# Storing zs before its silu and only q's rotated rows: a change to a one-core transformer-block kernel

## The chip, the cores and the metric

The kernel runs on one core of a Trainium2 chip. TensorE (PE) multiplies matrices, VectorE (DVE) and ScalarE (ACT) work element by element, GpSimd (POOL) mostly issues accumulating DMAs here, and SyncE (SP) issues most of the others; a DMA is carried by the core's 16 DMA engines. The metric is the device time of one execution in microseconds, the median of several runs: 925.65 us before the change.

## The reference

One block of a streaming encoder on 1024 tokens of width 1024, in float32. Cut to what matters (`h @ w_in` is split by columns into q, k, v, za, u, vs, zs and the gates gm):

```python
h = rmsnorm(x, norm_g)
q, k, v, za, u, vs, zs, gm = jnp.split(h @ w_in, IN_SPLITS, axis=-1)
q, k = partial_rope(q, pos), partial_rope(k, pos)   # rows 0..15 of each head's 64 turn, 16..63 stay
a = window_sink_attention(q, k, v, sinks)           # 16 heads of 64, 2 of them for k and v
a = (a * silu(za)) @ w_att_out
sgo = chunked_spatial_gating(gelu(u), gelu(vs), ...)
sgo = (sgo * silu(zs)) @ w_sg_out
ga, gs = jnp.split(sigmoid(gm + b_merge), 2, axis=-1)
x = rmsnorm(x + (ga * a + gs * sgo) @ w_o, final_g)
```

`partial_rope` takes x1 (the first eight rows of a head) and x2 (the next eight) and makes x1 cos - x2 sin and x2 cos + x1 sin.

## The kernel before, in words

Activations lie transposed: channels on the 128 partitions, tokens along the row, in two halves of 512. A big product is made in pairs of 128 channels (m and m + 1, m = 0, 2, 4, 6) by `gemm_pair`, which replaces eight block products by seven: b11, t1, t2, b21, t3, b22, t4 in this order. Each is 12 matmuls of 128x128 by 128x512, since every float32 operand is split into a high and a low part (`wh` on ACT, `wl` on DVE). Weights arrive as `wr`; their sums `s` are made on DVE (L242 to L245), one pair ahead, and split as well; t1 to t4 of the next pair need `wl<-s` and `wh<-s`. The results of a pair are four quarters x (128x512), put together on ACT (L359, L363, L366) and DVE (L371, L376, L380). `finish` is called for each quarter, and `hook` after each of the seven products: through hooks the side work (rotation, attention, loads ahead) is spread over the products. x tiles are reused, so a quarter must have left its tile before a later pair can fill it.

The stages in time: rmsnorm and vs (to about 100 us), u (107 to 218), k and v (218 to 238), q (four pairs, to 296), zs (four pairs, 296 to 429), gs and ga (eight pairs, to 610), za (four pairs, to 686), the product with w_sg_out (`sg`, to about 783), the product with w_att_out, the output product and the last norm.

**q.** `finish` puts each quarter twice: raw to `q_raw` in DRAM, and split into high and low parts (`split_q`, L880 on ACT, L882 on DVE) to `q_hl`, from where attention loads it. `rotate(g, pause)` does the 16 rotated rows for a group g of eight heads: it loads x1 and x2 from `q_raw` (L935, all eight heads, both halves of tokens, on 128 partitions), waits `1 + pause` hooks, multiplies by the tables (L955 to L957, L960 to L962) and puts the result over the rows in `q_hl` through `split_q`. Group 0 is rotated in the q pairs m = 4 and 6, group 1 in the first zs pair. `rotate` loads through SP's queue, which serves its issues in order; an issue that waits for a put to land holds up all that stand behind it.

**zs.** `zs_pair` collects the four raw quarters, then takes their silu on ACT (L1061), loads four factors of 256 KB from `s1_dr` (the mixed and gated branch, stored in the u stage), multiplies on DVE (L1071) and puts to `s_dr`. Attention runs beside the pairs m = 2, 4, 6 and beside gs and ga; its exponentials (L1120) and the silu use different activation tables on ACT, so ACT loads a table where they alternate (ACT_TABLE_LOAD). `exps` and `after` order silus behind the last exponentials.

**gs, ga.** They are stored by `rest(dst, m)`, which puts each raw quarter to `gs_dr` and `ga_dr` without activation.

**za.** `finish` takes the silu of each quarter (L1360), multiplies by a gate from `at_dr` (the attention's result, L1361) and puts to `a_dr`; four gates wait in the tag "g". From m = 2 on the four quarters of s (1 MB each) are loaded from `s_dr` into the tag "bq", and at m = 6 `forms_of` begins to make the operands T_ of the sg pairs from them on ACT and DVE.

Of the kernel before, what the change touches and what calls it, by code (L numbers as in the profile page):

```python
# [52 lines left out]
def hybrid_tile(  # L53
# [63 lines left out]
    q_raw = scratch("q_raw")  # L117
    q_hl = scratch("q_hl", (2, D, S))
# [4 lines left out]
    s_dr = scratch("s_dr")  # L123
# [751 lines left out]
    def split_q(src, places):  # L875

        hl = mtile([P, 2, HALF], F32R, "qhl", 3, pool)
        hi, lo = (hl[:, a, :].rearrange("p (t q c) -> p t c q", c=2, q=64) for a in range(2))
        src = src.rearrange("p (t c q) -> p t c q", c=2, q=64)
        nc.scalar.mul(hi, src, SC)  # L880
        for c in range(2):
            nc.vector.scalar_tensor_tensor(  # L882
                lo[:, :, c], src[:, :, c], SC, hi[:, :, c].bitcast(F32), op0=ALU.mult, op1=ALU.subtract
            )
        for at, dst in places:
            nc.sync.dma_start(dst, hl[at].bitcast(F32))
# [42 lines left out]
    def rotate(g, pause):  # L929

        x1, x2, a, b = (mtile([P, HALF], F32, "rot", 5, pool) for _ in range(4))
        for j, dst in enumerate((x1, x2)):
            src = q_raw[:].rearrange("(h d) t -> h d t", h=16)[8 * g : 8 * g + 8, 8 * j : 8 * j + 8]
            for half in range(2):
                nc.sync.dma_start(dst[halves[half]], src[:, :, half_of(half)])  # L935

        def split_rows(src, j):
# [4 lines left out]
                        (halves[half], a),  # L942
                        q_hl[a].rearrange("(h d) t -> h d t", h=16)[
                            8 * g : 8 * g + 8, 8 * j : 8 * j + 8, half_of(half)
                        ],
                    )
                    for a in range(2)
# [76 lines left out]
    def query_stage(g, t, par):  # L1024
# [3 lines left out]
        for j in range(2):  # L1028
            rows = q_hl[j].rearrange("(c r d) t -> r d c t", r=2, d=HD)[par]
            nc.sync.dma_start(  # L1030
                qt[j * HD : (j + 1) * HD].bitcast(F32), rows[:, 4 * g : 4 * g + 4, t * P : (t + 1) * P]
            )
# [3 lines left out]
    exps = []  # L1036
# [7 lines left out]
    def zs_pair(m, hook, *place, ahead_by=0):  # L1044
        quarters, fetched, hooked = [], [], [0]

        def fetch(i, half):
            fetched.append(get(s1_dr, m + i, half, *place))

        def step():  # L1050
            hook()
            hooked[0] += 1
            if hooked[0] == ahead_by:
                for at in ((0, 0), (1, 1)):
                    fetch(*at)

        gemm_pair(hb, lambda *quarter: quarters.append(quarter), step)

        first = None
        for i, half, q, src, sign in quarters:  # L1060
            silu = nc.scalar.activation(q[:], src, AF.Silu, scale=sign)  # L1061
            first = first or silu
            if silu is not first:
                after(silu, first)
            elif exps:
                after(silu, exps[-1])
        for i, half, q, src, sign in quarters:
            if not fetched:
                fetch(i, half)
            g = fetched.pop(0)  # L1070
            nc.vector.tensor_mul(q[:], q[:], g[:])  # L1071
# [17 lines left out]
    def softmax_stage(g, t, par, qt):  # L1089
# [40 lines left out]
        exps.append(nc.scalar.activation(es[:], es[:], AF.Exp))  # L1130
# [140 lines left out]
    QUARTERS = ((0, 0), (0, 1), (1, 0), (1, 1))  # L1271

    def loads_of_quarters(qs, src):


        def load(j, half):
            q = mtile([P, 4, HALF], F32, "bq", 4, pool)
# [23 lines left out]
    def load_o(name, wait=lambda move: None):  # L1301
        q = mtile([P, 4, HALF], F32, "bq", 4, pool)
# [41 lines left out]
    def want_gates(src, m):  # L1344
        for i, half in ORDER:
            gates.append(get(src, m + i, half, 4))


    for m in range(0, KC, 2):
        if m == 0:  # L1350
            want_gates(at_dr, m)
        if m == 2:
            s_q = {}
            ahead_of_time += loads_of_quarters(s_q, s_dr)
# [4 lines left out]
        def finish(i, half, q, src, sign):  # L1359
            nc.scalar.activation(q[:], src, AF.Silu, scale=sign)  # L1360
            nc.vector.tensor_mul(q[:], q[:], gates.pop(0)[:])  # L1361
# [4 lines left out]
        gemm_pair(hb, finish, part_of_loads, "tp")  # L1366
    want_gates(gs_dr, 0)
# [18 lines left out]
    for m in range(0, KC, 2):  # L1386
# [7 lines left out]
        def finish(i, half, q, src, sign):  # L1394
            gated(q, src, sign, gate_of(gs_dr, m, i, half, KC))
            put(y_dr, m + i, half, q[:], nc.gpsimd)
            gates.append(get(gs_dr, m + 2 + i, half, 4) if m < 6 else get(ga_dr, i, half, 4))
# [67 lines left out]
    for m in range(0, KC, 2):  # L1465
# [6 lines left out]
        def finish(i, half, q, src, sign):  # L1472
            gated(q, src, sign, gate_of(ga_dr, m, i, half, 0))
            if m < 6:
                add_to(place(y_dr, m + i, half), q[:])
                gates.append(get(ga_dr, m + 2 + i, half, 4))
# [23 lines left out]
    def load_rows(p):  # L1500
        xr = mtile([P, 4, HALF], F32, "bq", 4, pool)
# [6 lines left out]
    for p in range(4):  # L1508
        acc = bank("sc" if p < 2 else "mm")[:]
        x11 = mtile([P, HALF], F32, "g", 4, pool)  # L1510
# [5 lines left out]
    g_out = mtile([P, 4, HALF], F32, "bq", 4, pool)[:, 0:2, :]  # L1516
# [8 lines left out]
    for p in range(4):  # L1525
# [10 lines left out]
        def add_and_square(i, half, src, sign):  # L1536
# [4 lines left out]
            if p == 3 and i == half:  # L1541
                scaled[i, half] = mtile([P, HALF], F32, "g", 4, pool)
# [157 lines left out]
```

## Time and profile before

| | |
|---|---|
| median of 3 runs | 925.65 us (924.44 to 926.13) |
| the profiled execution | 928.16 us, of which the span of the profile is 926.4 us |
| TensorE's granted clock, mean | 0.994 of full speed |
| PE busy | 908.8 us (98%) |
| DVE, ACT, POOL busy | 691.7, 530.7, 127.0 us |
| chain that ended last | PE 79%, DVE 10%, ACT 4%, DMA 3% |
| DMA | 201.71 MB, mean 218 GB/s |

A row of a timeline reads: start and length in us, engine and line, operation, output<-input, shapes, count, and in brackets how long the engine stood idle before it and what it waited for. A row of waits reads: who waited, for whom, us in total, how many times, the longest. A granted clock of 1.00 is full speed; PE counts as busy at any clock. The share of DMA is a mean over the 16 engines.

### The profile page before, as it was taken

To read this page: it belongs to the slowest core of one execution; us is meant where nothing else is said; L and a number is where in the kernel's file an instruction comes from. 1 tells how busy PE (TensorE), PEld (TensorE's weight loads), DVE (VectorE), ACT (ScalarE), POOL (GpSimd) and SP (SyncE) were. 2 spreads that over 40 slices of the span, in tenths; PEclk is the share of its full clock that TensorE was granted. 3 is DMA by queue.
4 is the path that set the end of the run, shared out by engine and by line. 5 is a ranking of instruction groups with operands and counts; after the bars stand their busy time and mean duration, and the time that the engine had idled before them with its cause. 6 is when DMAs were issued, how large, how long until landed. Compare 5 with 4: busy or idle time off the path is not lost.

```text
span 926.4 us, 13211 instructions
## 1 busy us (share of the span) xinstructions
PE 908.8 (98%) x4332; PEld 754.6 (81%) x4332; DVE 691.7 (75%) x1245; ACT 530.7 (57%) x1057; POOL 127.0 (14%) x188
## 2 busy tenths in 40 slices
PE   8999999999999999999999999999999999999996
PEld 6888888888888778788888888888887887888885
DVE  6774776656687578888878888746498589579996
ACT  6862443334455468887666676744475475467443
POOL 0002122213021001101111121001100111110012
PEclk9999999999999989999999999999999999999999
DMA  6427678777788777888687789779668764998632
GB/s 239 136 90 208 208 199 182 164 157 233 231 294 269 210 222 196 223 212 231 188 228 258 233 175 258 209 263 323 217 199 325 256 197 151 298 313 282 205 114 114
DMA packets 128830, 201.71 MB, mean 218 GB/s; under 512 B 12441, under 2 KB 60825, under 8 KB 128762
## 3 DMA queue, kind: packets, MB, share of 16 engines
q1 hardware_dynamic: 109608, 148.17, 49.3%
q0 software_dynamic: 19008, 52.44, 23.6%
q8 instruction: 34, 0.56, 0.2%
q14 instruction: 34, 0.28, 0.1%
q10 hardware_dynamic: 146, 0.27, 0.1%
HBM read 144.07 MB, written 86.11 MB: 248 GB/s over the span
## 4 chain that ended last, share of the span: by engine, by line
PE 79%; DVE 10%; ACT 4%; DMA 3%; issue 3%; SPq 1%; DVEq 0%; ACTq 0%
PE ps_mm L341 32%; PE ps_o L341 23%; PE ps_mm L596 5%; PE ps_sc L1107 3%; PE ps_tp L341 2%; DVE wl L156 2%; PE ps_o L1192 2%; PE ps_sc L341 2%; PE ps_tp L1151 2%; PE ps_tp L764 2%; DVE bq L185 1%; PE ps_tp L565 1%; PE ps_sc L565 1%; PE ps_o L565 1%; PE ps_mm L565 1%
## 5 line engine op out<-in xcount | busy, mean ns | idle before, releaser
L155 ACT CAST wh<-s 128x1024 fp32r<-128x1024 f32 (+1 forms) x78 | 78.1, 1005 | 89.7 <-PE ps_mm L341 44.5
L156 DVE TENSOR_TENSOR wl<-wr,wh 128x1024 fp32r<-128x1024 f32 (+1 forms) x80 | 75.7, 947 | 56.0 <-ACT wh L155 55.3
L155 ACT CAST wh<-wr 128x1024 fp32r<-128x1024 f32 (+1 forms) x80 | 66.3, 830 | 76.1 <-PE ps_mm L341 37.3
L156 DVE TENSOR_TENSOR wl<-s,wh 128x1024 fp32r<-128x1024 f32 (+1 forms) x78 | 90.8, 1166 | 9.9 <-ACT wh L155 9.9
L341 PE MATMUL ps_o<-T_b22h,wh 128*128 128x512 f32 x148 | 58.7, 396 | 2.0 <-ACT x L363 2.0
L341 PE MATMUL ps_o<-T_t1h,wh 128*128 128x512 f32 x148 | 58.9, 398 | 0.3 <-ACT wh L155 0.2
L341 PE MATMUL ps_o<-T_b22h,wl 128*128 128x512 f32 x148 | 58.0, 392 | 0.0
L341 PE MATMUL ps_o<-T_t1h,wl 128*128 128x512 f32 x148 | 57.8, 391 | 0.2 <-DVE wl L156 0.2
L341 PE MATMUL ps_o<-T_b22l,wh 128*128 128x512 f32 x148 | 57.9, 391 | 0.0
L341 PE MATMUL ps_o<-T_t1l,wh 128*128 128x512 f32 x148 | 57.7, 390 | 0.0
L341 PE MATMUL ps_mm<-T_b11h,wl 128*128 128x512 f32 x140 | 54.8, 392 | 2.1 <-DVE wl L156 2.1
L341 PE MATMUL ps_mm<-T_t4h,wh 128*128 128x512 f32 x140 | 55.2, 394 | 1.1 <-DVE x L376 0.9
L341 PE MATMUL ps_mm<-T_t2h,wh 128*128 128x512 f32 x140 | 54.9, 392 | 1.2 <-ACT x L359 1.2
L341 PE MATMUL ps_mm<-T_t3h,wh 128*128 128x512 f32 x140 | 55.8, 399 | 0.0
L1120 ACT ACTIVATE pr<-ps_sc,sm 128x192 f32<-128x192 f32 (+2 forms) x128 | 50.9, 409 | 8.0 <-DVE sm L1116 7.0
L341 PE MATMUL ps_mm<-T_b11h,wh 128*128 128x512 f32 x140 | 55.0, 393 | 0.0
L341 PE MATMUL ps_mm<-T_t3l,wh 128*128 128x512 f32 x140 | 55.0, 393 | 0.0
L341 PE MATMUL ps_mm<-T_t3h,wl 128*128 128x512 f32 x140 | 54.9, 392 | 0.0
L341 PE MATMUL ps_mm<-T_t4h,wl 128*128 128x512 f32 x140 | 54.7, 391 | 0.0
L341 PE MATMUL ps_mm<-T_b11l,wh 128*128 128x512 f32 x140 | 54.6, 390 | 0.0
L341 PE MATMUL ps_mm<-T_t2l,wh 128*128 128x512 f32 x140 | 54.6, 390 | 0.0
L341 PE MATMUL ps_mm<-T_t2h,wl 128*128 128x512 f32 x140 | 54.6, 390 | 0.0
(358 smaller groups left out, 2413.8 us busy)
## 6 DMA issues: line engine op xcount, KB each, us to landing
wr<-in_w_dram SPq DMA_DIRECT2D x86, 256.0 KB
sums<-in_w_dram POOLq DMA_DIRECT2D x20, 512.0 KB, 6.1
s<-sums SPq DMA_DIRECT2D x20, 512.0 KB
s_dr<-x SPq DMA_DIRECT2D x32, 256.0 KB
q_hl<-qhl SPq DMA_DIRECT2D x16, 512.0 KB
q<-q_hl SPq DMA_DIRECT2D x64, 128.0 KB
wr<-in_w_dram SPq DMA_DIRECT2D x14, 512.0 KB
y_dr<-x POOLq DMA_DIRECT2D x28, 256.0 KB, 6.5
```

The costliest lines, as they stand in the source:

```text
L155: nc.scalar.copy(hi, src)
L156: return nc.vector.tensor_sub(lo, src, hi.bitcast(F32))
L185: op(dst[:, i : i + 2, :], a[:, i : i + 2, :], c[:, i : i + 2, :])
L341: nc.tensor.matmul(acc, lt, rt, start=fresh and k == 0 and n == 0, stop=k == 3 and n == 2, skip_group_check=True,)
L565: mm = nc.tensor.matmul(acc, lt, rt, start=k == 0 and n == 0, stop=k == KC - 1 and n == 2)
L596: nc.tensor.matmul(acc[:], lt, rt, start=k == 0 and n == 0, stop=k == KC - 1 and n == 2)
L764: nc.tensor.matmul(pm[:, t * P : (t + 1) * P], xh[:, half * 4 + t, g * P : (g + 1) * P], bias[-1][1][:, g % 4, :], start=True, stop=True,)
L1107: nc.tensor.matmul(sc[:, i, k0:], q_of[:, c, i * P : (i + 1) * P], kt[:, f, k0:], start=f == 0, stop=f == 1,)
L1120: nc.scalar.activation(held_in[c, i], sc[:, i, lo:hi], AF.Exp, bias=nmax[:, c, i : i + 1], scale=-1.0, accum_out=sums[:, c, i : i + 1],)
L1151: nc.tensor.transpose(dst, pr[:, i, block * P : block * P + width], ident[:])
L1192: nc.tensor.matmul(po[:, cs], lt, rt, start=n == 0, stop=n == len(terms) - 1)
```

## The change

- Of q, `finish` stores to `q_raw` only the 16 rows of each head that turn, in a layout of (first or second eight rows, half of the tokens, 128 rows, 512 tokens), as two DMAs of 32 KB (one for each head of the quarter) in place of one of 256 KB. `q_hl` has a row's high and low part of a half next to each other, so that its puts have rows of 4 KB; a rotation makes two puts of it per result in place of four.
- `rotate` makes two loads (x1 and x2, 256 KB each) in place of four of 128 KB. Group 1 is rotated one hook later (`rotate(1, 2)`), and attention's first loads are a step of their own beside it.
- The zs pairs store raw quarters to `z_dr` by `rest`, as gs and ga do. `zs_pair`, `exps` and the order of silus behind exponentials are gone.
- The za pairs do what was left out: `parts_of_s` loads the four quarters of z (1 MB each) and the factors of s1 (two of 1 MB for rows 0 to 511, eight of 256 KB by rows for the rest), takes silus of 128x1024, and multiplies, at the places of a table (m, product). za's own multiply and put come at a later hook (`finish_silu`); gates use two of four buffers, the row factors the other two.

```diff
-    q_raw = scratch("q_raw")
-    q_hl = scratch("q_hl", (2, D, S))
+    q_raw = scratch("q_raw", (2, 2, P, HALF))
+    q_hl = scratch("q_hl", (D, 2, 2, HALF))
...
         for j, dst in enumerate((x1, x2)):
-            src = q_raw[:].rearrange("(h d) t -> h d t", h=16)[8 * g : 8 * g + 8, 8 * j : 8 * j + 8]
-            for half in range(2):
-                nc.sync.dma_start(dst[halves[half]], src[:, :, half_of(half)])
+            nc.sync.dma_start(dst[:], q_raw[j, :, 64 * g : 64 * g + 64])
...
-            put(q_raw, m + i, half, q[:])
+            for head in range(2):
+                at = 8 * (2 * (m + i) + head)
+                copy_to(q_raw[:, half, at : at + 8, :], q[head * HD : head * HD + 16, :])
             rows = slice((m + i) * P, (m + i + 1) * P)
-            split_q(q[:], [(slice(0, P), q_hl[:, rows, half_of(half)].rearrange("a p t -> p a t"))])
+            split_q(q[:], [(slice(0, P), q_hl[rows, half].rearrange("p a t -> p (a t)"))])
...
-        first = None
-        for i, half, q, src, sign in quarters:
-            silu = nc.scalar.activation(q[:], src, AF.Silu, scale=sign)
...
-        for i, half, q, src, sign in quarters:
-            if not fetched:
-                fetch(i, half)
-            g = fetched.pop(0)
-            nc.vector.tensor_mul(q[:], q[:], g[:])
-            put(s_dr, m + i, half, q[:])
-
-    steps_of_q += [rotate(1, 1), first_loads()]
-    zs_pair(0, part_of_q, 5, "rot")
+    steps_of_q.append(rotate(1, 2))
+    q_loads = first_loads()
+
+    def beside_zs():
+        part_of_q()
+        next(q_loads, None)
+
+    gemm_pair(hb, rest(z_dr, 0), beside_zs)
...
-    for m in range(2, KC, 2):
-        zs_pair(m, lambda: part_of_attention(m == 2), 2, ahead_by=3)
-    for dst in (gs_dr, ga_dr):
-        for m in range(0, KC, 2):
-            gemm_pair(hb, rest(dst, m), part_of_attention)
+    for dst in (z_dr, gs_dr, ga_dr):
+        for m in range(2 if dst is z_dr else 0, KC, 2):
+            gemm_pair(hb, rest(dst, m), lambda: part_of_attention(dst is z_dr and m == 2))
...
+        def silu(j, half):
+            for c in range(0, 4, 2):
+                v = s_q[j, half][:, c : c + 2, :]
+                after(nc.scalar.activation(v, v, AF.Silu), pace[0])
+
+        def multiply(j, half, c):
+            v = s_q[j, half][:, c : c + 2, :]
+            after(nc.vector.tensor_mul(v, v, factors[-1][:, c : c + 2, :]), term[0])
...
+        def multiply_row(c, half):
+            v = s_q[1, half][:, c, :]
+            after(nc.vector.tensor_mul(v, v, of_rows[c, half][:]), term[0])
+
+        return {
+            (0, 1): [(load, 0, 0), (load_factors, 0, 0)],
+            (0, 2): [(load, 1, 1)],
+            (0, 3): [(load, 0, 1)],
...
+            (4, 7): [(multiply_row, 0, 0), (multiply_row, 1, 0), (load_row, 2, 0), (load_row, 3, 0)],
+            (6, 3): [(multiply_row, 2, 0), (multiply_row, 3, 0)],
+        }
...
         def finish(i, half, q, src, sign):
-            nc.scalar.activation(q[:], src, AF.Silu, scale=sign)
-            nc.vector.tensor_mul(q[:], q[:], gates.pop(0)[:])
-            put(a_dr, m + i, half, q[:], nc.gpsimd)
-            if m < 6:
-                gates.append(get(at_dr, m + 2 + i, half, 4))
+            pace[0] = nc.scalar.activation(q[:], src, AF.Silu, scale=sign)
+            silus.append((q, m + i, half))
```

What the change moves shows in three places. First DVE in the first zs pair, before (`wr` and `s` are weights and their sums, `wl` their low parts, `rot` the tiles of the rotation, `qhl` the split rows, `x` the quarters):

```order
L371 TENSOR_TENSOR x_2592<-x_2592,ps_o_2658 128x512
L955 TENSOR_TENSOR rot_2610<-rot_2608,tab_308_2070 128x512
L156 TENSOR_TENSOR wl_2673<-wr_2583,wh_2672 128x1024
L956 TENSOR_TENSOR rot_2611<-rot_2609,tab_320_2126 128x512
L961 TENSOR_TENSOR rot_2608<-rot_2608,tab_320_2126 128x512
L957 TENSOR_TENSOR rot_2610<-rot_2610,rot_2611 128x512
L960 TENSOR_TENSOR rot_2609<-rot_2609,tab_308_2070 128x512
L376 TENSOR_TENSOR x_2594<-x_2594,ps_mm_2591 128x512
```

And the same place of the change, to the first split of a sum:

```order
L376 TENSOR_TENSOR x_2604<-x_2604,ps_mm_2601 128x512
L950 TENSOR_TENSOR rot_2620<-rot_2618,tab_308_2074 128x512
L951 TENSOR_TENSOR rot_2621<-rot_2619,tab_320_2131 128x512
L956 TENSOR_TENSOR rot_2618<-rot_2618,tab_320_2131 128x512
L952 TENSOR_TENSOR rot_2620<-rot_2620,rot_2621 128x512
L955 TENSOR_TENSOR rot_2619<-rot_2619,tab_308_2074 128x512
L380 TENSOR_TENSOR x_2603<-x_2603,ps_o_2629 128x512
L882 SCALAR_TENSOR_TENSOR qhl_2685<-rot_2620,qhl_2685 128x256 x2
L957 TENSOR_TENSOR rot_2619<-rot_2619,rot_2618 128x512
L243 TENSOR_TENSOR s_2599<-s_2599,wr_2593 128x512
L244 TENSOR_TENSOR s_2600<-wr_2593,wr_2594 128x512
```

L376, which stood behind five instructions of the rotation, stands ahead of all of them; L380 and the sums of the next pair's weights stand behind five of them, as the sums did.

SP's queue at the end of the q stage, before, from the last quarters of q to attention's first loads:

```order
L457 DMA q_raw<-x_2421 128x512
L886 DMA q_hl<-qhl_2546 128x2x512
L457 DMA q_raw<-x_2571 128x512
L886 DMA q_hl<-qhl_2574 128x2x512
L200 DMA wr_2584<-in_w_dram 128x512
L935 DMA rot_2608<-q_raw 64x1x512 x2
L935 DMA rot_2609<-q_raw 64x1x512 x2
L1030 DMA q_2702<-q_hl 64x4x128 x2
```

And of the change:

```order
L200 DMA q_raw<-x_2431 2x8x512
L886 DMA q_hl<-qhl_2555 128x1024
L200 DMA q_raw<-x_2580 2x8x512 x2
L886 DMA q_hl<-qhl_2584 128x1024
L200 DMA wr_2594<-in_w_dram 128x512 x2
L933 DMA rot_2618<-q_raw 128x1x512
L933 DMA rot_2619<-q_raw 128x1x512
L996 DMA k_2624<-k_dr 128x2x128
L1028 DMA q_2626<-q_hl 64x4x128 x2
```

The rotation's loads keep their place behind the last put of q_raw and a load of weights; they are fewer and larger, and their source has its rows in two parts (one for each half of the tokens).

ACT behind the products of the first zs pair, before:

```order
L366 COPY x_2593<-ps_mm_2591 128x512
L155 CAST wh_2672<-wr_2583 128x1024
L1061 ACT_TABLE_LOAD
L1061 ACTIVATE x_2592<-x_2592 128x512
L880 ACTIVATE qhl_2650<-rot_2610 128x4x2x64
L1061 ACTIVATE x_2594<-x_2594 128x512
L880 ACTIVATE qhl_2679<-rot_2609 128x4x2x64
L1061 ACTIVATE x_2593<-x_2593 128x512
```

And of the change:

```order
L366 COPY x_2603<-ps_mm_2601 128x512
L155 CAST wh_2678<-wr_2593 128x1024
L880 ACTIVATE qhl_2685<-rot_2620 128x4x2x64
L469 ACTIVATE x_2748<-ps_mm_2601 128x512
L880 ACTIVATE qhl_2708<-rot_2619 128x4x2x64
L155 CAST wh_2732<-s_2599 128x1024
```

The table load and the silus are gone from this place; L469 copies the last raw quarter.

More of the change, by code (lines that the diff above doesn't have):

```diff
@@ L122, in hybrid_tile @@
     s1_dr = scratch("s1_dr")
-    s_dr = scratch("s_dr")
+    z_dr = scratch("z_dr")
     gs_dr = scratch("gs_dr")
@@ L941, in split_rows @@
                     (
[L942 to L945, printed above, removed]
+                        halves[half],
+                        q_hl[:, half].rearrange("(h d) a t -> h d (a t)", h=16)[8 * g : 8 * g + 8, 8 * j : 8 * j + 8],
                     )
-                    for a in range(2)
                     for half in range(2)
@@ new lines, in hybrid_tile, with finish_silu, part_of_s @@
+    of_att = [(m + i, half) for m in range(0, KC, 2) for i, half in ORDER]
+    s_q = {}
+    making_s = parts_of_s()
+    of_za = [0]
+    silus = []
+    def finish_silu(q, m, half):
+        after(nc.vector.tensor_mul(q[:], q[:], gates.pop(0)[:]), term[0])
+        put(a_dr, m, half, q[:], nc.gpsimd)
+        if of_att:
+            want_gate(at_dr, *of_att.pop(0), 2)
+    def part_of_s(m):
+        of_za[0] += 1
+        if of_za[0] % 7 not in (2, 3, 4) and silus:
+            finish_silu(*silus.pop(0))
+        for f, *args in making_s.get((m, (of_za[0] - 1) % 7 + 1), ()):
+            f(*args)
@@ L1349, in hybrid_tile @@
     for m in range(0, KC, 2):
         if m == 0:
[L1351 to L1354, printed above, removed]
+            for _ in range(2):
+                want_gate(at_dr, *of_att.pop(0), 2)
         if m == 6:
```

84 lines of the change are left out of this document (48 added, 36 removed).

## The prediction

> **What bounds the kernel now.** I read the page first, then who TensorE (PE) waited for, then the places of the long waits.
>
> ```profile
> span 926.4 us, 13211 instructions
> PE 908.8 (98%) x4332; PEld 754.6 (81%) x4332; DVE 691.7 (75%) x1245; ACT 530.7 (57%) x1057; POOL 127.0 (14%) x188
> ```
>
> PE is busy for 908.8 of 926.4 us, and the change leaves its matmuls alone, so it can only take away PE's waits, or add some. A tenth of a microsecond on DVE or ACT is worth nothing unless PE stands still for it. The answer on PE's waits has these rows (total, times, longest):
>
> ```profile
> PE ps_mm L341 <- DVE wl L156: 2.1, 2, 1.1
> PE ps_o L341 <- ACT x L363: 2.0, 1, 2.0
> PE ps_sc L498 <- DVE T_b22l L494: 1.9, 1, 1.9
> PE ps_mm L341 <- ACT x L359: 1.2, 2, 0.9
> PE ps_mm L341 <- DVE x L376: 0.9, 1, 0.9
> ```
>
> The first and third lie at changes of stage and aren't aimed at. The other three lie in the zs pairs (296 to 429 us). Their places on PE:
>
> ```profile
> 296.16 0.39 PE L341 MATMUL ps_mm<-T_b11h,wh 128*128 128x512 f32 x1
> ...
> 314.04 0.50 PE L341 MATMUL ps_mm<-T_t4h,wh 128*128 128x512 f32 x1 [0.95 <-DVE x L376]
> ...
> 330.52 0.50 PE L341 MATMUL ps_o<-T_b22h,wh 128*128 128x512 f32 x1 [2.05 <-ACT x L363]
> ...
> 381.75 0.50 PE L341 MATMUL ps_mm<-T_t2h,wh 128*128 128x512 f32 x1 [0.93 <-ACT x L359]
> ```
>
> The wait of 2.05 us costs more than itself, as the stretches around it show (columns: length, then busy time of PE, PEld, DVE, ACT, POOL, granted clock, DMA share, GB/s):
>
> ```profile
> 325.00:330.00 5.00, 3.48 (x16) 2.54 (x14) 3.14 (x5) 0.75 (x2) 0.00 (x0) 1.00 0.70 236
> 330.00:335.00 5.00, 4.42 (x16) 3.47 (x17) 4.85 (x18) 4.59 (x14) 0.00 (x0) 0.68 0.83 275
> 335.00:340.00 5.00, 5.00 (x21) 4.19 (x21) 3.75 (x13) 3.52 (x17) 0.00 (x0) 0.64 0.65 195
> 345.00:420.00 75.00, 73.47 (x389) 61.00 (x388) 63.06 (x144) 63.56 (x162) 11.77 (x14) 1.00 0.81 212
> 420.00:600.00 180.00, 180.00 (x986) 154.65 (x985) 147.71 (x347) 128.54 (x366) 23.95 (x32) 1.00 0.80 223
> ```
>
> Right behind the wait the clock is 0.68 and 0.64: 5 x 0.32 + 5 x 0.36 = 3.4 us of work lost while PE counts as busy. The last row is what zs pairs become: from 420 us gs and ga pairs run beside the same attention, stored raw, and PE never waits in 180 us.
>
> By the Trainium skill ("TensorE: Matmul & The Clock Gate", Part 1) the clock halves after an idle window of about 3.4 us; here it fell behind a wait of 2.05 us, so the measurement decides, and any new wait of that length may cost the 3.4 us again.
>
> **The change, part by part.**
>
> *Raw zs: what goes.* Why those waits stand, on DVE first, then on ACT:
>
> ```profile
> 310.89 0.69 DVE L956 TENSOR_TENSOR rot<-rot,tab 128x512 f32<-128x512 f32 x1 [1.11 <-DMA rot<-q_raw]
> ...
> 317.65 1.22 DVE L156 TENSOR_TENSOR wl<-s,wh 128x1024 fp32r<-128x1024 f32 x1
> ...
> 326.07 0.69 DVE L1071 TENSOR_TENSOR x<-x,rot 128x512 f32<-128x512 f32 x1 [5.78 <-DMA rot<-s_dr]
> ```
>
> ```profile
> 329.87 0.60 ACT L363 ACTIVATE x<-ps_o 128x512 f32<-128x512 f32 x1 [3.68 <-DMA s_dr<-x]
> ...
> 377.08 1.28 ACT L1061 ACT_TABLE_LOAD   x1
> ```
>
> At 330.52 PE waits for L363, which waits for an x tile, which waits for a put of s_dr, which waits for L1071 and so for factors loaded late. The change has no such multiply there, and z_dr is put as soon as x is summed: 2.05 + 3.4 us gone. At 381.75 (and once more, 1.2 in all) L359 stands behind a table load and silus of L1061; both go: 1.2 us. At 314.04 L376 stands behind rotation multiplies that wait for their load; in the change L376 stands ahead of them: 0.95 us. Next behind these on every engine is the gs picture above, without waits. Sum: 2.05 + 3.4 + 1.2 + 0.95 = 7.6 us.
>
> *Rotated rows alone.* Each of the 16 quarters of q puts two pieces of 32 KB (2x8x512, one for each of its two heads) in place of one 128x512 of 256 KB, and each rotation makes two loads of 256 KB in place of four of 128 KB. Both new forms have an outermost axis of only two steps on one side (the first and second eight rows of a head; in the loads, half of the tokens). The trace has no transfer of 256 KB in this form, so I bound it. From the chain (start, length, what):
>
> ```profile
> 285.44 2.73 PE ps_o L341 x12
> ...
> 299.44 4.38 DMA q_raw<-x
> ...
> 303.88 0.62 SPq L935
> ...
> 305.87 4.93 DMA rot<-q_raw
> ...
> 321.11 7.11 DMA rot<-s_dr
> ...
> 328.96 1.91 DMA s_dr<-x
> ```
>
> and from the stretches:
>
> ```profile
> 255.00:262.00 7.00, 7.00 (x33) 5.79 (x32) 6.44 (x11) 4.70 (x7) 0.00 (x0) 1.00 1.00 356
> 262.00:303.90 41.90, 41.90 (x187) 34.69 (x186) 30.68 (x53) 19.34 (x29) 8.73 (x16) 1.00 0.82 274
> 313.50:318.50 5.00, 4.46 (x20) 3.68 (x21) 5.00 (x10) 3.82 (x6) 0.00 (x0) 1.00 0.42 138
> ```
>
> Lower end: the loads spread over all engines and land when they did, at 305.87 + 4.93 = 310.8. Upper end: a transfer goes as no more streams than that axis has steps, two engines of the 16. One engine moves 356 / 16 = 22.3 GB/s where all are full (255 to 262), so 128 KB on each takes 131,072 / 22.3 = 5.9 us; both loads on the same two engines 11.8 us. Issued from 303.9, straight behind the landing of the last put (299.44 + 4.38 = 303.8) as before, second issue at 304.5 (0.62 each), with 1.9 us for the way (the shortest transfer of the chain): landed at 304.5 + 11.8 + 1.9 = 318.2.
>
> Backlog can make it later still. Between 262 and 303.9 the engines are 0.82 busy, so one has 41.9 x 0.18 = 7.5 us free. The two engines would get, for eight quarters, 32 KB each in place of 16 KB (1.47 for 0.74 us, 5.9 us more) and group 0's loads (11.8 for 1.5 us, 10.3 more): 16.2 - 7.5 = 8.7 us behind by 303.9. Then the landing is at 318.2 + 8.7 = 326.9. Everything on SP's queue has a share on those engines; before the end of pair m=6 that would show in the sums behind wr (L242).
>
> Near which end? SP's own issues in that last stretch are these:
>
> ```profile
> 313.52 5.13 SPq L886 DMA_DIRECT2D q_hl<-qhl  x8
> ```
>
> It issues eight 8x8x512 puts, and the mean share falls to 0.42 although the load behind them took 7.11 us: a form with a short outer axis leaves engines empty while others are late. This row is nearer to the upper end, and I take it, with half the backlog (part of it runs off while PE stands): about 322.5.
>
> The Trainium skill ("DMA: Bandwidth & Descriptors", Why a DMA increments its semaphore by 16 and not by 1) states that a transfer runs on the largest number of engines up to 16 that divides the slowest axis of both sides, and always on the lowest ones; for these forms that is the same two engines. By it the landing is at 318 or later, and by a full spread at 310.8; no view here counts the engines of one transfer.
>
> *What the late load costs.* In before, DVE needs 310.89 to 317.65 + 1.22 = 318.87, 8.0 us, from the first rotation multiply behind the landed load to the first wl<-s. The change queues the same things behind its loads: five multiplies and sums of the rotation, L380, the splits, L243, L245, then wl<-s for the next pair's t1. PE needs that wl: b11 at 296.16 plus seven products of 2.72 is 315.2 for the next b11, 317.9 for t1, whose third matmul reads wl at 318.4. So the load must have landed by 310.4. Landed at 310.8: 0.4 us of wait. At 318.2: 7.8. At 326.9: 16.5. At 322.5: 12.1 us, in one or two waits. One wait of that size costs the half clock again, 3.4 us by the rows at 330 (none at the least, twice that if pair m=6 stalls as well). The rotation's place one product later only moves L376 and the wait: what was a wait of t4 for L376 is now one of t1 for wl.
>
> *The za stage.* It gets what zs lost, 8 silus of 128x1024 in place of 16 of 128x512, 4 + 8 multiplies, 4 MB of factors. Rows that bear on it:
>
> ```profile
> 600.00:690.00 90.00, 90.00 (x409) 74.72 (x409) 55.24 (x66) 47.08 (x65) 10.01 (x18) 1.00 0.72 246
> 670.00:690.00 20.00, 20.00 (x90) 16.57 (x89) 18.10 (x20) 17.32 (x22) 2.50 (x5) 1.00 0.57 192
> 690.00:710.00 20.00, 18.83 (x82) 14.97 (x81) 20.00 (x22) 11.76 (x15) 1.82 (x4) 1.00 0.87 302
> ```
>
> ```profile
> L1361 DVE TENSOR_TENSOR x<-x,g 128x512 f32<-128x512 f32 x16 | 10.9, 685 | 1.5 <-DMA wr<-in_w_dram 0.7 <-ACT x L1360 0.7
> ...
> L185 DVE TENSOR_TENSOR bq<-bq,bq 128x1024 f32<-128x1024 f32 x4 | 4.9, 1219 | 0.0
> ```
>
> Multiplies: 8 x 0.685 + 4 x 1.22 = 10.4 us on DVE, which is idle for 90 - 55.2 = 34.8 us there; the silus are 8 pieces on an ACT idle for 42.9 us. Hidden, but for the end: two row multiplies (1.4 us) fall into pair m=6, where DVE has 1.9 us of 20 left, ahead of the forms of s that DVE makes without a pause from 690. Bounds 0 and 1.4 us; I take 0.5, since 1.4 fits in 1.9. The 4 MB at 274 GB/s are 15 us of transfers, with 90 x 0.28 = 25 us free: nothing.
>
> Sum: -7.6 + 12.1 + 3.4 + 0.5 = +8.4 us. Against the profiled execution (926.4 of span, 1.76 around it, 928.16) that is 936.6; this execution lies 2.5 us over the median of 925.65, and the difference is put on the median: 934.
>
> **The rivals.**
>
> *The loads spread evenly.* For it: the four loads before landed 4.93 us after the last issue, and the change has half the issues and a quarter of the bytes to put. Against: the 0.42. It gives -7.6 + 0.4 + 0.5 = -6.7, 919. This is the other side, one mechanism with its place: rotation of group 1 at 304 to 311 us. It decides at a landing of 310.4 + about 4 = 314: there the wait with its half clock eats the gain.
>
> *Two engines, but no backlog, and the clock holds.* -7.6 + 7.8 + 0.5 = +0.7, 926.4; with the half clock +4.1. For it: share 0.64 to 0.82 leaves room; against: 16.2 us more for 7.5 free.
>
> *Full backlog, two falls of the clock.* -7.6 + 16.5 + 6.8 + 0.5 = +16.2, 942.
>
> *The gain isn't there.* The waits in zs go because work leaves; the gs stretch shows it. Only if za's end pays with a wait of 2 us and a fall of the clock (2 + 3.4) is the gain of the first rival down to 1.3 us; 690 to 710 shows PE waiting 1.17 us already without a fall of the clock, against it.
>
> **How the numbers follow.** A measurement of this kernel tells about 0.2% from no change, 1.85 us. Late loads with part of the backlog (+2 to +13): 0.50. Full backlog: 0.10. Two engines without backlog: 0.12, of which 0.08 is within 0.2% and 0.03 above, 0.01 below. Even spread: 0.25, faster. Gain eaten at za's end: 0.03, half of it within 0.2%. So faster 0.27, same 0.10, slower 0.63. The range goes from the even spread, 918, to most of the full backlog, 941; the likeliest case alone is 928 to 939.
>
> **What would show it.** Right: PE's list of waits without L363, L359 and L376, clock 1.00 between 345 and 420; a wait of PE of 6 us or more for wl or s near 318 to 325, behind DVE waiting for DMA rot<-q_raw, the clock below 0.8 behind it; perhaps a wait near 292 to 300 behind wr. Wrong: DVE's first rotation multiply of group 1 starts before 312 us and PE never waits over 1 us between 280 and 330; then the loads did spread, and the time is about 919. A new wait over 1.5 us at 686 to 710 would show the price of za too low.

## The result, and the profile after

The change takes 948.74 us (948.07 to 948.8, 4 runs) where the kernel before takes 925.89 (924.44 to 928.07, 4 runs): ratio 1.0243, 95% interval 1.0222 to 1.0264. It is slower by 22.9 us; forecast were +8.4 and 934, with 941 as the upper end. The profiled execution's span is 947.0 us against 926.4, and its page begins:

```profile
span 947.0 us, 13164 instructions
## 1 busy us (share of the span) xinstructions
PE 914.5 (97%) x4332; PEld 759.3 (80%) x4332; DVE 690.2 (73%) x1241; ACT 521.6 (55%) x1046; POOL 127.1 (13%) x188
```

PE's idle time grew from 926.4 - 908.8 = 17.6 to 947.0 - 914.5 = 32.5 us, 14.9 more, and the same 4332 matmuls took 5.7 us longer, at a mean granted clock of 0.982 in place of 0.994. The two make the 20.6 us of the spans; the medians lie 22.9 apart because the profiled execution of the kernel before was 2.3 us over the median of 925.89. PE's waits, with the same columns as before:

```profile
PE ps_o L341 <- DVE wl L156: 6.5, 2, 5.8
PE ps_sc L1078 <- DMA q<-q_hl: 5.5, 1, 5.5
PE ps_mm L341 <- DVE x L376: 3.9, 2, 3.5
PE ps_mm L341 <- DVE wl L156: 2.6, 2, 1.5
PE ps_o L341 <- ACT wh L155: 2.5, 1, 2.5
```

None of them is one of those that the change was to take away: L363 and L359 are gone from the list, and the wait for L376 is another one, in the za stage. Where they stand on PE:

```profile
285.62 0.80 PE L341 MATMUL ps_o<-T_t1h,wl 128*128 128x512 f32 x1 [5.80 <-DVE wl L156]
...
331.66 1.94 PE L1078 MATMUL ps_sc<-k,q 128*128 128x128 f32 x8 [5.52 <-DMA q<-q_hl]
...
336.12 0.79 PE L341 MATMUL ps_o<-T_t1h,wh 128*128 128x512 f32 x1 [2.53 <-ACT wh L155]
338.00 0.80 PE L341 MATMUL ps_o<-T_t1h,wl 128*128 128x512 f32 x1 [0.66 <-DVE wl L156]
...
698.29 0.80 PE L341 MATMUL ps_mm<-T_t4h,wh 128*128 128x512 f32 x1 [3.46 <-DVE x L376]
...
723.64 0.50 PE L341 MATMUL ps_mm<-T_b11h,wl 128*128 128x512 f32 x1 [1.50 <-DVE wl L156]
```

The first matmul behind a wait takes 0.80 us at half clock and 0.50 at full clock (the row at 723.64). The stretches show it in the column of the granted clock:

```profile
285.00:290.00 5.00, 4.38 (x10) 3.47 (x11) 4.94 (x9) 1.84 (x4) 4.06 (x8) 0.50 0.70 189
290.00:295.00 5.00, 5.00 (x21) 4.06 (x20) 1.46 (x3) 2.26 (x4) 0.00 (x0) 0.88 0.76 225
...
332.00:338.00 6.00, 2.82 (x11) 1.91 (x10) 5.97 (x12) 4.28 (x6) 0.00 (x0) 0.50 0.38 115
338.00:343.00 5.00, 5.00 (x13) 3.97 (x14) 1.20 (x1) 0.39 (x1) 0.00 (x0) 0.56 0.69 207
...
380.00:440.00 60.00, 60.00 (x333) 51.85 (x332) 49.77 (x117) 43.20 (x123) 8.31 (x10) 1.00 0.80 210
...
695.00:700.00 5.00, 1.71 (x4) 1.42 (x5) 5.00 (x7) 4.60 (x6) 0.54 (x1) 0.74 0.23 73
700.00:705.00 5.00, 5.00 (x14) 3.89 (x14) 3.40 (x5) 3.37 (x6) 1.08 (x2) 0.58 0.56 163
...
725.00:730.00 5.00, 5.00 (x17) 3.90 (x16) 4.13 (x6) 0.56 (x1) 1.10 (x3) 0.69 1.04 388
```

Idle time plus busy time times what the clock lacks, by place: q pair m=6, 5.8 + 4.38 x 0.50 + 5 x 0.12 = 8.6 us; first zs pair, 5.52 + 2.53 + 0.66 + 2.82 x 0.50 + 5 x 0.44 = 12.3; za, 3.46 + 1.71 x 0.26 + 5 x 0.42 = 6.0; the change from za to sg, 1.50 + 5 x 0.31 = 3.1, where before had 1.17 and no fall of the clock. Together 30.0 - 1.2 - 7.6 (the waits that went) = 21.2, near the 20.6 of the spans. From 380 to 440 us zs pairs run with no wait, as forecast.

What PE waits for at 285 and 326 to 338 is, in the end, two loads. On DVE, the first two multiplies of group 1's rotation:

```profile
324.01 0.69 DVE L950 TENSOR_TENSOR rot<-rot,tab 128x512 f32<-128x512 f32 x1 [5.32 <-DMA rot<-q_raw]
...
329.96 0.69 DVE L951 TENSOR_TENSOR rot<-rot,tab 128x512 f32<-128x512 f32 x1 [5.25 <-DMA rot<-q_raw]
```

The loads were issued one behind the other from 314.95 on and landed 5.95 us apart. If each runs on two engines, that is 131,072 bytes per engine in 5.95 us, or 22.0 GB/s, close to the 22.3 that the forecast worked out for one engine: the two ran one after the other on the same two engines. The kept trace bears this out: its records of DMA packets show about two packets of 2 KB (a row of these loads) under way at a time from 317.2 to 327.5 us (mean 2.2). In the stages from q to the first zs pair the 16 engines were 0.53 busy on the mean (166 GB/s, 262 to 345). The chain shows who stood behind them (start, length, what):

```profile
273.87 9.12 DMA q_hl<-qhl
...
283.09 0.63 ACT qhl L155
...
284.35 1.23 DVE wl L156
285.62 4.64 PE ps_o L341 x10
...
316.14 3.93 SPq L996
...
320.12 11.00 DMA q<-q_hl
```

A put of 512 KB that took 5.1 us before (5.09 in the chain at 291.36) takes 9.12 behind group 0's loads, its tile is free late, the split that wants the tile holds ACT and DVE, and t1 of pair m=6 waits for its wl. At 320 one of attention's first loads of q takes 11.0 us behind group 1's.

### The profile page after: what moved, and what is told of

Read it like the earlier page. It is cut to its first block, busy times and chain, and to the rows that moved or that the text cites. A ratio compares the mean times of both kernels' runs of the same rounds, so it can differ in the third digit from the quotient of the medians.

```text
span 947.0 us, 13164 instructions
## 1 busy us (share of the span) xinstructions
PE 914.5 (97%) x4332; PEld 759.3 (80%) x4332; DVE 690.2 (73%) x1241; ACT 521.6 (55%) x1046; POOL 127.1 (13%) x188
## 4 chain that ended last, share of the span: by engine, by line
PE 78%; DMA 7%; DVE 7%; issue 3%; ACT 2%; SPq 2%; DVEq 0%; ACTq 0%
PE ps_mm L341 32%; PE ps_o L341 24%; PE ps_mm L596 4%; PE ps_sc L1078 3%; PE ps_o L1163 2%; PE ps_tp L1122 2%; DMA wr<-in_w_dram 2%; PE ps_sc L341 2%; DMA q<-q_hl 2%; PE ps_tp L341 2%; PE ps_tp L764 2%; DVE wl L156 1%; DMA bq<-g 1%; PE ps_tp L565 1%; PE ps_sc L565 1%
## 5 line engine op out<-in xcount | busy, mean ns | idle before, releaser
L341 PE MATMUL ps_o<-T_t1h,wl 128*128 128x512 f32 x148 | 60.1, 406 | 6.5 <-DVE wl L156 6.5
L341 PE MATMUL ps_mm<-T_t4l,wh 128*128 128x512 f32 x140 | 56.1, 400 | 0.0
```

Source lines behind the costliest of these rows:

```text
L341: nc.tensor.matmul(acc, lt, rt, start=fresh and k == 0 and n == 0, stop=k == 3 and n == 2, skip_group_check=True,)
```

## The experiments

Four theories were to be told apart. *Streams*: a transfer runs on as many engines as its outermost axis allows, so loads with an axis of two are slow and all that follows on SP's queue with them. *Order*: the new order on DVE and SP, or the longer rows of q_hl, make the waits. *Moved zs*: the work moved to za is the loss. And for za: late factor rows, or too much for DVE.

**flat_loads.** Only the layout changes, so that a load's source is one axis of 128 rows:

```diff
-    q_raw = scratch("q_raw", (2, 2, P, HALF))
+    q_raw = scratch("q_raw", (2, 2, 2, 64, HALF))
-            nc.sync.dma_start(dst[:], q_raw[j, :, 64 * g : 64 * g + 64])
+            nc.sync.dma_start(dst[:], q_raw[j, g].rearrange("a r t -> (a r) t"))
-                copy_to(q_raw[:, half, at : at + 8, :], q[head * HD : head * HD + 16, :])
+                copy_to(q_raw[:, at // 64, half, at % 64 : at % 64 + 8, :], q[head * HD : head * HD + 16, :])
```

> The change, with one thing altered: q_raw is laid out so that the 128 rows that a rotation loads lie in one run (one axis of 128 in the source in place of two axes of 2 and 64). Number, size and order of all transfers stay. Theory (a transfer runs on few engines when its outermost axis is short): the loads land within 6 us of their issue, PE's waits of 5.8 us at 285 and of 5.5 and 2.5 us at 326 to 338 fall under 1 us each, and the time is 926 to 931. Rival (the order on DVE and SP, the rotation one product later, or the longer rows of q_hl make the waits): nothing changes, 946 to 950.

Measured: 931.24 us (1.0051 of before, 1.0033 to 1.007), 0.2 over the upper end of what was expected. DVE's two multiplies follow each other without a wait:

```profile
312.06 0.68 DVE L950 TENSOR_TENSOR rot<-rot,tab 128x512 f32<-128x512 f32 x1
312.66 0.68 DVE L951 TENSOR_TENSOR rot<-rot,tab 128x512 f32<-128x512 f32 x1
```

PE's long waits from 280 to 338 are gone but for one of another kind, at attention's first step, with a fall of the clock behind it:

```profile
PE ps_sc L1078 <- ACT pr L1091: 2.6, 1, 2.6
...
330.00:335.00 5.00, 4.99 (x21) 4.17 (x22) 3.96 (x14) 4.61 (x21) 0.00 (x0) 0.66 0.78 166
```

A put of 512 KB takes 5.54 us here, at 286, and the packet records show about 15 packets of 2 KB, other transfers' among them, under way at a time while the rotation's loads are out (308.2 to 311). Count, size and order of the transfers are those of the change, so 17.5 us hang on one axis. Order falls as their cause; of the 3.8 us that are left over z_alone (below) it may still hold a part.

**four_axis.** The same with four steps in the load's outermost axis:

```diff
-    q_raw = scratch("q_raw", (2, 2, P, HALF))
+    q_raw = scratch("q_raw", (2, 4, 2, 32, HALF))
-            nc.sync.dma_start(dst[:], q_raw[j, :, 64 * g : 64 * g + 64])
+            nc.sync.dma_start(dst[:], q_raw[j, :, g])
...
-                copy_to(q_raw[:, half, at : at + 8, :], q[head * HD : head * HD + 16, :])
+                row = 64 * half + at % 64
+                copy_to(q_raw[:, row // 32, at // 64, row % 32 : row % 32 + 8, :], q[head * HD : head * HD + 16, :])
```

> The change with q_raw laid out so that a rotation's load has four steps on its outermost axis (4 x 32 rows) in place of two; count, size and order stay. Theory (as many streams as steps): 64 KB on each engine, 2.9 us a load in place of 5.9, the second load lands 7 to 10 us after its issue (14.4 in the change, about 5 with one axis of 128), and the time lies between the kernel with flat loads (931) and the change (949): 932 to 940. Rival (any axis but a single run of 128 is slow, or only the axis of two is a special case): 946 to 950, or 931.

Measured: 938.77 us (1.015, 1.0128 to 1.0172). The multiplies on DVE:

```profile
317.57 0.69 DVE L950 TENSOR_TENSOR rot<-rot,tab 128x512 f32<-128x512 f32 x1 [3.42 <-DMA rot<-q_raw]
...
320.76 0.69 DVE L951 TENSOR_TENSOR rot<-rot,tab 128x512 f32<-128x512 f32 x1 [2.50 <-DMA rot<-q_raw]
```

They stand 3.2 us apart where 64 KB on one engine take 2.9, and two steps gave 5.95: the time of a load goes with the steps of that axis. Four packets of 2 KB are under way at a time from 311.5 to 318 (mean 4.3). Streams holds by its number.

**by_head.** Layout by head, so that puts have an axis of 16 and loads one of 8 (four loads of 128 KB):

```diff
-    q_raw = scratch("q_raw", (2, 2, P, HALF))
+    q_raw = scratch("q_raw", (2, 2 * P, HALF))
...
-            nc.sync.dma_start(dst[:], q_raw[j, :, 64 * g : 64 * g + 64])
+            for half in range(2):
+                src = q_raw[half].rearrange("(h d) t -> h d t", h=16)[8 * g : 8 * g + 8, 8 * j : 8 * j + 8]
+                nc.sync.dma_start(dst[halves[half]], src)
...
-                copy_to(q_raw[:, half, at : at + 8, :], q[head * HD : head * HD + 16, :])
+                copy_to(q_raw[half, 2 * at : 2 * at + 16, :], q[head * HD : head * HD + 16, :])
```

> The change, with q_raw laid out by head: a put has 16 rows on its outermost axis in place of 2, a rotation loads four times eight heads by eight rows (128 KB) as the kernel before did. Theory (short outermost axis): loads and puts both spread, so no wait of PE over 1 us is left from 262 to 345 and the time is 924 to 929; against the variant with flat loads alone it shows what the puts cost, 0 to 3 us. Rival (order of the queues): 946 to 950; rival (fewer, larger loads matter, not the axis): as the kernel with flat loads does not improve, this one does.

Measured: 930.66 us (1.004, 1.0025 to 1.0055), a little above the 924 to 929 expected: PE's wait near 330 stays, 2.4 us, where none over 1 us was expected. Its loads lie in eight pieces in DRAM, so one run of memory, as in flat_loads, is not what a fast load needs. Against flat loads, 0.6 us lies within the intervals: short puts and the split of the loads together cost nothing that can be told.

**head_both.** The same kernel in one more execution. 

> The variant by head again, one look, as it was: does its wait near 325 to 332 and the clock behind it repeat (2.4 us, 0.80 and 0.86)? Theory: the wait repeats, the fall of the clock behind a wait of 2 to 3 us comes in some executions only. Rival: it comes each time.

 Measured: 930.55 us; the wait was 2.7 us and the clock 0.54 and 0.77 in the ten microseconds around and behind it (0.80 and 0.86 in by_head). Both repeat in these two executions; whether the fall comes in each, two can't tell.

**q_alone.** The kernel before with q's part of the diff and nothing else. 

> The kernel before with only q's part of the change (rotated rows alone, layouts of q_raw and q_hl, two loads); zs keeps its silu, its multiply and the rotation at its old product. Theory (q's transfers are the loss): 940 to 952, with PE's waits near 285 and after 312. Rival (the moved zs work is the loss): 924 to 929.

Measured: 952.02 us (1.0265, 1.0239 to 1.0291). PE's longest waits:

```profile
PE ps_o L341 <- DVE wl L156: 6.9, 2, 6.2
PE ps_sc L1103 <- DMA q<-q_hl: 6.6, 1, 6.6
```

q's part alone costs more than the whole change costs, about 25 us, at the upper end of what was expected.

**z_alone.** The change with q's part undone. 

> The change without q's part: q_raw and q_hl are stored and loaded as before, the rotation one product later, zs raw and its silu and multiply beside za. Theory (q's transfers are the loss): the zs waits of 7.6 us are gone, za costs 6 to 8 us with its wait for the last factor rows, so 923 to 929. Rival (the moved zs work is the loss): 944 to 950.

Measured: 927.46 us (1.0007, 0.9997 to 1.0017): no change that can be told. Its waits show where part of the gain went:

```profile
PE ps_mm L341 <- DVE x L376: 3.0, 1, 3.0
PE ps_sc L1082 <- ACT pr L1095: 3.0, 1, 3.0
PE ps_mm L341 <- DVE wl L156: 2.8, 2, 1.7
```

The three waits of the zs pairs are gone, and two of 3.0 us have come: in za, and at attention's first step at 325 us. Moved zs as the great loss falls.

**z_rows.** z_alone with za's table pulled forward; the second factors are multiplied at (2, 4) and (2, 5) and not at (2, 6) and (2, 7), and so on down the table:

```diff
-            (2, 1): [(multiply_row, 0, 1), (multiply_row, 1, 1), (load_row, 2, 1), (load_row, 3, 1)],
-            (2, 3): [(silu, 0, 1)],
-            (2, 6): [(multiply, 0, 1, 0), (multiply_row, 2, 1)],
-            (2, 7): [(multiply, 0, 1, 2), (multiply_row, 3, 1), (load, 1, 0), (load_row, 0, 0), (load_row, 1, 0)],
-            (4, 6): [(silu, 1, 0)],
-            (4, 7): [(multiply_row, 0, 0), (multiply_row, 1, 0), (load_row, 2, 0), (load_row, 3, 0)],
-            (6, 3): [(multiply_row, 2, 0), (multiply_row, 3, 0)],
+            (2, 1): [(multiply_row, 0, 1), (multiply_row, 1, 1), (load_row, 2, 1), (load_row, 3, 1), (silu, 0, 1)],
+            (2, 4): [(multiply, 0, 1, 0)],
+            (2, 5): [(multiply, 0, 1, 2), (load, 1, 0)],
+            (2, 6): [(multiply_row, 2, 1), (multiply_row, 3, 1), (load_row, 0, 0), (load_row, 1, 0)],
+            (4, 3): [(silu, 1, 0)],
+            (4, 4): [(multiply_row, 0, 0), (multiply_row, 1, 0), (load_row, 2, 0), (load_row, 3, 0)],
+            (6, 1): [(multiply_row, 2, 0), (multiply_row, 3, 0)],
```

> The change without q's part, with the za table pulled forward: the second factors are multiplied two products earlier, so that the last quarter of z and the last factor rows are loaded 5 to 8 us earlier. Theory (za's wait of 3.0 us for L376 comes from DVE standing behind the last row multiplies, whose factors landed 8.8 us after a late issue, and the forms of s behind them): DVE's wait for the last factors falls from 4.3 to under 1 us, PE's wait for L376 near 680 goes, the clock stays 1.00 there, and the time falls by 3 to 6 us against the same kernel without it (927.5), to 922 to 925. Rival (DVE has too much to do between 665 and 700, whenever the rows come): under 1 us.

Measured: 924.54 us (0.9979, 0.9968 to 0.9991), within the 922 to 925 expected and 2.9 under z_alone (2.6 by the ratios, since the two ran beside different executions of the kernel before), where 3 to 6 were expected. It is the first version whose interval lies under the kernel before, by 0.2%. In the change DVE waited here for the last factors (the profile writes s1_dr as s_dr) and then had the forms of s ahead of L376:

```profile
688.33 1.29 DVE L1359 TENSOR_TENSOR bq<-bq,g 128x512 f32<-128x512 f32 x2 [4.28 <-DMA g<-s_dr]
...
697.56 0.68 DVE L376 TENSOR_TENSOR x<-x,ps_mm 128x512 f32<-128x512 f32 x1
```

and the chain has the load ahead of it:

```profile
679.55 8.76 DMA g<-s_dr
```

With the table pulled forward the za stage is nearly whole:

```profile
600.00:690.00 90.00, 89.80 (x396) 73.83 (x394) 64.43 (x76) 54.47 (x72) 9.45 (x17) 1.00 0.85 299
```

DVE has 64 us of work in these 90 and PE waits 0.2; DVE's wait of 4.28 us for the last factors is not among its waits there. So za's price was when the factors were asked for, not how much DVE has to do.

**head_rows.** by_head with the same table. 

> The variant by head with the za table pulled forward. Theory (za's wait is the late last factor rows, whatever q does): 2 to 4 us under the variant by head (930.6), 926.5 to 928.5; and about 3 us over the same with q stored whole (924.5), which then is the price of q's rows in themselves. Rival (q's rows cost nothing, the difference of 3 us was the clock's luck): 923.5 to 925.

 Measured: 926.65 us (1.0014, 1.0001 to 1.0027), 4.0 under by_head (2.4 by the ratios) and 2.1 over z_rows (3.2 by the ratios, whose intervals do not meet). Storing q's rows alone costs some 2 to 3 us even when it is spread; where these arise was not followed.

**z_late.** z_alone with attention's first two parts two hooks later, to see whether the first step only starts too early. 

> The change without q's part, attention's first two parts left out of the first two hooks beside zs pair m = 2 (they run later, nothing is dropped). Theory (PE's wait of 3.0 us for the first exponentials at 325 comes from an attention that starts before its tiles are free of the rotation, whose last put landed at 322): that wait falls under 1 us and the time by 2 to 5 us, to 922.5 to 925.5. Rival (the first step of attention costs its chain of DVE, table load and ACT wherever it starts): the wait stays at 2 to 3 us, 927.

Measured: 937.69 us (1.0119, 1.0097 to 1.0142). The gain did not come: the wait at attention's first step stays (2.2 us), and eight waits of another kind come:

```profile
PE ps_o L1167 <- DVE x L371: 7.5, 8, 1.8
```

Two hooks are not a whole step of attention (three parts), so its value matmuls fell on products that use their bank.

**z_both.** z_late with the table. 

> Both together: za's table pulled forward and attention two hooks later, q stored and loaded as before. If both theories hold the gains add: 918 to 922, faster than the kernel before (926.9) by 5 to 9 us, which is the 7.6 us of the zs waits, nearly whole. If only one holds: 922 to 925.

 Measured: 935.73 us (1.0106, 1.0076 to 1.0137). The 918 to 922 expected were not to be had, since z_late was a loss; the two intervals overlap.

**z_third.** z_rows with attention three hooks later:

```diff
-        for _ in range(1 if first else PARTS[of_pair[0] % 7]):
+        for _ in range((of_pair[0] > 3) if first else PARTS[of_pair[0] % 7]):
```

> The change without q's part, za's table pulled forward, attention three hooks later. Two hooks later cost 10 us, with eight waits of PE in attention's value step for the bank that the quarters use; its three steps then fell on other products. Three hooks is a whole step, so the places stay. Theory (attention starts before its tiles are free of the rotation): the wait of 2.4 us at 322 and the fall of the clock behind it go, 920 to 922.5. Rival (the first step costs its own chain of DVE, table load and ACT wherever it starts): the wait of 2 to 3 us stays, 924 to 926.

 Measured: 926.33 us (0.9996, 0.9984 to 1.0008). The eight waits are gone, the one at the first step is there, at 335 and 3.2 us long:

```profile
335.36 1.97 PE L1082 MATMUL ps_sc<-k,q 128*128 128x128 f32 x8 [3.19 <-ACT pr L1095]
```

That the step only starts too early falls.

**z_table.** z_rows with one idle exponential ahead, so that ACT's table is loaded before the first step. 

> The change without q's part, za's table pulled forward, and one exponential of a 128x1 tile in the first zs pair, whose result nobody uses, so that ACT loads the table of the exponentials there and not ahead of attention's first step. Theory (the wait of 2.4 us at 322 is the first step's own chain, DVE's maxima, then a table load of 1.28 us, then the exponentials): the wait falls to about 1.1 us, a fall of the clock behind it gets rarer, and the time goes from 924.5 to 921 to 923.5. Rival (the chain waits for memory that the rotation's last put frees, the table load lies beside it): the wait stays over 2 us and the time at 924 to 925.

 Measured: 924.57 us (0.9977, 0.9967 to 0.9987), as z_rows. The exponentials began at 322.84 right behind DVE's maxima, with no table load between, and PE waited 2.5 us all the same. So the table load alone is not the wait. The test is not clean: against z_rows the maximum came 0.6 us later (321.91 for 321.33), and the scores that wait stand four matmuls (0.9 us) earlier on PE, and these two eat the 1.28 us that the table load took. Ahead of its first maximum DVE stood idle:

```profile
321.91 0.62 DVE L1098 TENSOR_REDUCE sm<-ps_sc 128x2 f32<-128x128 f32 x2 [2.53 <-DMA z_dr<-x]
```

A landing of a put frees it, by this row; in z_third the same maximum came without idle time, behind weight sums and splits on DVE, with a table load behind it. Which of these would have to go stays open.

## Why the prediction was wrong, point by point

**The sign and the mechanism** were right: the rotation's loads ran as two streams, one after the other, at 22.0 GB/s where 22.3 was worked out, and 5.95 us apart where 5.9 was.

**The steps that failed** are two in the sum of -7.6 (waits that go), 12.1 + 3.4 (the late loads) and 0.5 (za). The price of za was put at 0.5 us and measured 7.9, because a load comes too late and not because DVE has too much to do. And what stands behind the waits that go was put at nothing, where flat_loads shows 2.6 us of wait and 1.7 us by the clock. By place in the profiles the sum is -7.6 + 20.9 + 7.9 = 21.2 us, where 8.4 was forecast. By terms:

- *The za stage*, 0.5 us with bounds 0 and 1.4, is the largest miss: it cost 6.0 there and 1.9 more at the change to sg. DVE's spare time was the right number for the work (z_rows: no wait over 0.2 us with the same work), but not for its due time: the last rows' loads were issued at 679.55, took 8.76 us, and DVE stood for 4.28 us ahead of the forms of s. The change's own table could have told it: these loads stand at (4, 7), behind the multiplies that free their tiles, and what they feed at (6, 3), three products or 8.2 us later, which is less than the load took. The sentence "a new wait over 1.5 us at 686 to 710 would show the price of za too low" came true, with 3.46.
- *What stands behind the waits that go* was put at nothing: "the gs picture above, without waits". But in each of the nine other kernels without the wait for L363 and without loads of two or four streams, attention's first step makes PE wait, 2.2 to 3.2 us (2.6 in flat_loads, 3.0 in z_alone), mostly with a fall of the clock. That the wait for L363 had covered it in the kernel before is argued, not tested.
- *The late loads*, 12.1 + 3.4 = 15.5 us, measured 8.6 + 12.3 = 20.9 in the two stretches. But flat_loads, whose loads are spread, still loses 5.4 there: waits of 0.8, 0.3 and 2.6 us and 1.7 by the clock, most of it at attention's first step. That leaves 15.5 us for the short axis by place, and 17.5 by the medians, against the 15 that the forecast had between its main case (934) and the even spread (919); q_alone puts it at 25, in the kernel with the old zs pairs. So the size of this term was near, but by luck, since it is made up of other parts than "half the backlog" and one wait.

**How the late loads' time is made up:**

- The backlog did not run off while PE stood; it was paid in two waits. SP's own waits say how (262 to 340):

```profile
SPq L200 <- DMA rot<-q_raw: 4.7, 1, 4.7
...
SPq L457 <- DMA rot<-q_raw: 2.5, 1, 2.5
```

  SP stood for 4.7 us until a load of group 0 had landed, so q's puts went out later, PE stood in pair m=6 (8.6 us with the clock), q's last quarters came later by that, and group 1's loads were issued from 314.95 on, not from 303.9: 11 us late at issue, where 8.7 was the full backlog and 4.3 was taken. From there the 11.8 us of the two loads came on top in full.
- The first wait ended at 285.62, 6.4 us ahead of "292 to 300 behind wr", and came by another way: by the tiles of the split rows, which a late put holds. That put was costed nowhere. A price was given for what reads the late load, none for the transfers that merely share its engines.
- Attention's first scores were left out of the path. They stand on PE ahead of t1 and wait for loads of q which run behind the rotation's loads: 5.52 us for q, then 2.53 + 0.66 for wh and wl, where only the wl was counted. This changed the wait's name more than its end: the wl that t1's third matmul reads came at 338.0, 8.0 us behind DVE's multiply at 329.96, as long as the chain that was forecast.

**The clock** fell behind both waits, by 2.8 and 3.6 us. That is the 3.4 of each, and twice, as the rival had it; the forecast counted it once.

**What the change removes** was right for the waits of zs: L363, L359 and L376 are gone there, and PE is whole from 380 to 440. But 3.4 of the 7.6 us were a fall of the clock in the one profiled execution, whose mean clock was 0.994. Of the 64 executions of this kernel beside the experiments only 6 had 0.994 (median 928.0 us), and 44 had 0.997 to 0.999 (the 29 at 0.998: median 925.8). For the median only 4.2 us were there to be won. The forecast took the 8.4 from the profiled execution and put it on the median; had it stayed with the profiled execution, it would have been 936.6. This, za and attention's first step are why not even half of the gain showed in z_alone.

**The rivals.** Even spread (919) did not come by itself; flat_loads made it come, and gave 931, not 919, for the most part because of za, the first step and the fall of the clock that the median does not have. No backlog with the clock holding, at 926.4, is refuted by 8.6 us of loss in q pair m=6. Full backlog with two falls of the clock, at 942, came nearest, with 23.3 us for the loads' two stretches, where 20.9 were measured. The rival that had the gain eaten at za's end by "a wait of 2 us and a fall of the clock (2 + 3.4)", given a chance of 0.03, is what happened there: 3.46 us of wait and 2.5 by the clock.

## What to carry to other kernels

Look at the outermost axis of both sides of every large transfer: four loads of 256 KB with an axis of two cost 17.5 us here, at 0.53 mean load of the engines, and a layout that makes this axis long takes these away. Price a slow transfer by all that shares its engines and its queue (puts that hold tiles, the next issues, the next stage's loads), not by its reader alone. Before a wait is booked as a gain, look whether the next step behind it is ready, and whether the clock's part of it is in the usual execution or only in the profiled one. And work that is moved into idle time has to be asked for early enough: ask of each moved step when its last load can be issued, which the release of a buffer may set, and what stands behind it on the same engine.

## What the runs showed of the hardware

- Load time by steps of the outermost axis, 256 KB each, second after first: 5.95 us at 2 steps, 3.2 at 4, no gap that DVE saw at 128; packets of 2 KB under way at a time: about 2, 4 and 15. The Trainium skill ("DMA: Bandwidth & Descriptors", Why a DMA increments its semaphore by 16 and not by 1) states that a transfer runs on the largest number of engines, at most 16, that divides the slowest axis of both sides. The runs agree with it.
- SP's queue can stand while earlier transfers are out: in the change 4.7 us, ahead of a put of q_raw, and 2.5 us, ahead of a put of z_dr, each until a load of the rotation had landed, by the profile. The put of z_dr reads and writes nothing of the rotation.
- The clock fell to 0.50 behind a wait of 5.8 us, to 0.58 behind one of 3.46 and to 0.69 behind one of 1.50; in head_both it was 0.54 in the stretch of a wait of 2.7 us, and in z_alone, behind one of 3.0 us at 325, it stayed at 1.00. In the kept traces half clock comes in stretches of 3.41, 6.83 or 13.65 us, but for the one at each trace's end. A wait of 1.5 to 3 us may or may not cost it, which is worth 1.5 to 3.6 us each time.
